# A two-layer hybrid transformer block: tail steps by banks, sums of squares on GpSimd, the inverse's matrices on VectorE, more turns for differential attention

## The chip, the cores and the metric

The kernel runs on one core of one Trainium2 chip. The metric is the device time of one execution in microseconds, as the median of several runs. A core has TensorE (PE in the profile, its weight loads PEld), VectorE (DVE), ScalarE (ACT), GpSimd (POOL) and SyncE (SP), which issues the DMAs. Each engine executes its own instructions in a fixed order and waits on semaphores for the others.

## The reference

x is 256 tokens by 1024. Each of two layers applies a feed-forward block, a mixer and a second feed-forward block, each with a norm before and a norm after it:

```python
for l in range(DEPTH):
    h = _rms_norm(x, ffn1_norm_pre[l])
    x = x + 0.5 * _rms_norm(_swiglu(h, ...), ffn1_norm_post[l])
    h = _rms_norm(x, mix_norm_pre[l])
    m = _mixer(h, w_in[l], ...)          # z = h @ w_in; three branches; gates; @ w_out
    x = x + _rms_norm(m, mix_norm_post[l])
    h = _rms_norm(x, ffn2_norm_pre[l])
    x = x + 0.5 * _rms_norm(_swiglu(h, ...), ffn2_norm_post[l])
```

`_swiglu` is `(silu(h @ w_gate) * (h @ w_up)) @ w_down` with an inner width of 2816. The mixer's branches are a sparse attention (top 64 keys by an index score), a linear recurrence (RWKV-7: a 64x64 state per head, updated by one rank-one correction per token), and differential attention: two softmaxes per head, p1 - lam * p2, times v, and a norm. All is float32.

## The kernel before, in words

**Tiling.** The 256 tokens are two halves t = 0 and 1 of 128. A matmul with weights of 512 or 1024 columns is cut into steps of 1024 weight values per partition. Each step's weights arrive by DMA in `raw`, and are split into a high part `wh` (a cast on ScalarE) and a rest `wl` (a subtraction on VectorE), both at line 224. A product is three matmuls, lines 233 to 235 (`mm3`): high by low, high by high, and `wl` by high. An output of 1024 columns fills two PSUM banks of 512.

**Order of steps.** `run_skew` (line 238) walks through a list of steps. The first `head` ones run for t = 0 and then for t = 1, the middle ones for both t in turn, and the last `tail` ones for t = 0 and then for t = 1. The last matmul of each stage (w_down, or w_out in a mixer) has a tail of EXTRA = 7 steps, whose weights are held for both t in extra buffers. A step of the tail does both banks before the next step. So t = 0 has its norm calculated while t = 1 is still multiplied. The transposes that the next stage needs (`rest`, line 356, PE line 362) are put into PE's order by `later`, ahead of the last step.

**Stage end.** `post_norm` (line 384) calls `rstd` (line 323): two squares with sums on ScalarE (line 330), their sum on VectorE (332), a power on GpSimd (333). Then for each half `y = ps * rstd * g` (391) and `x = y * factor + x` (392). `pre_norm` repeats `rstd` on the new x and makes `xn` (353), which PE transposes.

**The mixer's middle.** Three generators are advanced by `tick`, one turn after each step: sparse attention, differential attention (`diff`, line 740) and the recurrence. The recurrence inverts triangular matrices in `rwkv_solve` (line 996). After a small solve on VectorE and a passage through DRAM (`zs`, `xs`), four block-diagonal matrices `Z` are built on VectorE (line 1032), and two matrices `T` on GpSimd (1036) in the same turns as the first two Z. Then come three levels: `L` by Z on PE (line 193 through `mm`), masked to `W` on VectorE (1063), T by W on PE, and the addition to Z (1074). `diff` makes scores on PE, adds a mask (767), has a softmax over ScalarE and VectorE (653 to 656), combines both maps (773, 774) and, after LAG = 2 turns, transposes `lm` (line 196 through `tpose`) for the product with v. It does so for two head pairs of t = 0 and then of t = 1.

A scheduler puts instructions into each engine's order by priority: norms first (`pn`), weight loads and splits next (`p0`), then the generators' work (`p1`); `behind` keeps some of them after a given instruction.

Of the kernel before, what the change touches and what calls it, by code (L numbers as in the profile page):

```python
# [8 lines left out]
F32 = mybir.dt.float32  # L9
# [3 lines left out]
OP = mybir.AluOpType  # L13
# [6 lines left out]
EPS = 1e-6  # L20
# [3 lines left out]
LAG = 2  # L24
# [15 lines left out]
class Block:  # L40
# [197 lines left out]
    def run_skew(self, steps, head=0, tail=0):  # L238

        n = len(steps)  # L240
        order = [(t, i) for t in range(2) for i in range(head)]
        order += [(t, i) for i in range(head, n - tail) for t in range(2)]
        order += [(t, i) for t in range(2) for i in range(n - tail, n)]
        held = {}
        for j, (t, i) in enumerate(order):
            if self.later and (head and j == head - 1 or tail and j == len(order) - 1):
                self.later.pop(0)()
            if t == 0:
                wait = RING <= i < head or i >= n - tail
                held[i] = steps[i][0](self.extra if wait else self.ring)  # L250
            steps[i][1](t, held[i])
            self.tick()

    def steps_b(self, rows, n, ksteps, xk, psum, done=None):

        per = max(1, min(1024 // n, ksteps))
        steps, ps, raws = [], {}, {}
        nb = (n + 511) // 512

        def mk(k0):  # L260
            def ld(pool):
                if k0 % (2 * per) == 0:
                    kk = min(2 * per, ksteps - k0)
                    raws[0] = self.load(rows(k0, kk), kk, n)
                o = k0 % (2 * per)
                return self.split(raws[0][:, o:o + per, :], per, n, pool)

            def go(t, w):
                if k0 == 0:
                    ps[t] = [psum() for _ in range(nb)]  # L270
                for kk in range(per):
                    xh, xl = xk(k0 + kk, t)
                    for b in range(nb):
                        c0, c1 = b * 512, min(n, b * 512 + 512)
                        self.mm3(ps[t][b][:, :c1 - c0], xh, xl, w[0][:, kk, c0:c1], w[1][:, kk, c0:c1],
                                 k0 + kk == 0, k0 + kk == ksteps - 1, False)
                if k0 + per == ksteps and done is not None:
                    done(t, ps[t])
            return ld, go

        for k0 in range(0, ksteps, per):
            steps.append(mk(k0))
        return steps
# [39 lines left out]
    def rstd(self, parts, width):  # L323

        nc = self.nc
        ss = self.st.tile([128, 2], F32, name="ss")
        s = 1.0 / math.sqrt(width)
        for i, p in enumerate(parts):
            j = self.sq.tile([128, 512], mybir.dt.bfloat16, name="junk")
            nc.scalar.activation(j, p, AF.Square, scale=s, accum_out=ss[:, i:i + 1])  # L330
        r = self.st.tile([128, 1], F32, name="rstd")
        nc.vector.tensor_scalar(r, ss[:, 0:1], ss[:, 1:2], EPS, op0=OP.add, op1=OP.add)
        nc.gpsimd.tensor_tensor(r, r, self.mhalf[:, 0:1], op=OP.pow)
        return r

# [48 lines left out]
    def post_norm(self, t, ps, g, factor):  # L384
        nc = self.nc
        with self.pn():
            r = self.rstd(ps, D)
            for h in range(2):
                s = slice(h * 512, h * 512 + 512)
                y = self.junk.tile([128, 512], F32, name="xn")  # L390
                nc.vector.scalar_tensor_tensor(y, ps[h], r, g[:, s], op0=OP.mult, op1=OP.mult)
                nc.vector.scalar_tensor_tensor(self.x[t][:, s], y, factor, self.x[t][:, s], op0=OP.mult, op1=OP.add)
                if not self.phases:
                    nc.sync.dma_start(self.out[0, t * 128:t * 128 + 128, s], self.x[t][:, s])
        self.pre_norm(t)
# [344 lines left out]
    def diff(self, st, vd):  # L740
        nc = self.nc
        while "attended" not in st:
            yield
        q, k = st["dq"], st["dk"]
# [6 lines left out]
        for t in range(2):  # L751
# [5 lines left out]
            for h2 in range(2):  # L757
                lm = self.tp.tile([128, 1024], F32, name="lm", tag="lm", bufs=1)[:, :4 * S].rearrange(
                    "p (j s) -> p j s", s=S)
                yield  # L760
                pss = [self.bank(self.atp)[:, :2 * S].rearrange("p (j s) -> p j s", s=S) for _ in range(2)]
                for j in range(2):
                    for mp in range(2):
                        rw = slice(mp * 64, mp * 64 + 64)
                        self.mm(pss[mp][:, j, :], q[rw, 2 * h2 + j, ts], k[rw, 2 * h2 + j, :S], start=True, stop=True)
                for mp, ps in enumerate(pss):
                    nc.vector.scalar_tensor_tensor(lm[:, 2 * mp:2 * mp + 2, :], ps, 0.125,
                                                   self.cmS[:, None, o:].to_broadcast([128, 2, S]),
                                                   op0=OP.mult, op1=OP.add)
                rs = self.softmax(lm, 4, S, "d")  # L770
                for j in range(2):
                    p0, p1 = lm[:, j, :], lm[:, 2 + j, :]
                    nc.vector.tensor_scalar(p1, p1, rs[:, 2 + j:3 + j], lam, op0=OP.mult, op1=OP.mult)
                    nc.vector.scalar_tensor_tensor(p0, p0, rs[:, j:j + 1], p1, op0=OP.mult, op1=OP.subtract)
                for _ in range(LAG):
                    yield
                for s in range(t + 1):
                    yield
                    ps = self.bank(self.atp)[:, :256].rearrange("p (h c) -> p h c", c=128)
                    for j in range(2):  # L780
                        self.tpose(ps[:, j, :], lm[:, j, s * 128:s * 128 + 128], self.ident)
                    nc.scalar.copy((pt1 if s else pt0)[:, 2 * h2:2 * h2 + 2, :], ps)
# [7 lines left out]
            ss = self.st.tile([128, 4], F32, name="dss")  # L790
# [6 lines left out]
            for h in range(4):  # L797
                nc.vector.scalar_tensor_tensor(yt[:, h, :], ps[:, h, :], ss[:, h:h + 1], self.sub,
                                               op0=OP.mult, op1=OP.mult)
            yts.append(yt)  # L800
        for _ in range(2 * LAG):
            yield
        while self.gp is None:
# [192 lines left out]
    def rwkv_solve(self, Ls, strip):  # L996
# [32 lines left out]
        for q in range(4):  # L1029
            Zs.append(self.ep.tile([128, 4, 128], F32, name="Z", tag="s"))  # L1030
            with self.behind(self.attended):
                nc.vector.tensor_tensor(Zs[q].rearrange("p u (g x) -> p u g x", x=16),
                                        zs[:, 4 * q:4 * q + 4, None, :].to_broadcast([128, 4, 8, 16]), d16, op=OP.mult)
            if q < 2:
                Ts.append(self.ep.tile([128, 4, 128], F32, name="T", tag="s"))
                nc.gpsimd.tensor_tensor(Ts[q].rearrange("p v (g x) -> p v g x", x=16),
                                        xs[:, 4 * q:4 * q + 4, None, :].to_broadcast([128, 4, 8, 16]), even, op=OP.mult)
            yield


# [228 lines left out]
```

## Time and profile before

| what | value |
|---|---|
| median of 3 runs | 1435.26 us (1435.07, 1435.26, 1437.74) |
| the profiled execution's own time | 1437.46 us |
| its span in the profile | 1435.8 us |
| busy: PE, DVE, ACT, POOL | 1399.8, 1012.3, 713.2, 77.5 us |
| chain that ended last | PE 79%, DVE 9%, DMA 6%, ACT 3%, issue 2% |
| HBM traffic | 171 GB/s over the span |

Layer 0's mixer builds its Z at 362 us, layer 1's at 1072 us. Feed-forward and mixer stages end at about 197, 532, 718, 906, 1241 and 1430 us (the first five by the first transposes, line 362, of the next). The rows in the section below are single instructions or groups. In a timeline row a bracket gives the idle time of the engine before it and what ended it; in a table by stretches, "PEclk" is the granted TensorE clock as a share of full speed.

### The profile page before, as it was taken

To read this page: it belongs to the slowest core of one execution; us is meant where nothing else is said; L and a number is where in the kernel's file an instruction comes from. 1 tells how busy PE (TensorE), PEld (TensorE's weight loads), DVE (VectorE), ACT (ScalarE), POOL (GpSimd) and SP (SyncE) were. 2 spreads that over 40 slices of the span, in tenths; PEclk is the share of its full clock that TensorE was granted. 3 is DMA by queue.
4 is the path that set the end of the run, shared out by engine and by line. 5 is a ranking of instruction groups with operands and counts; after the bars stand their busy time and mean duration, and the time that the engine had idled before them with its cause. 6 is when DMAs were issued, how large, how long until landed. Compare 5 with 4: busy or idle time off the path is not lost.

```text
span 1435.8 us, 20311 instructions
## 1 busy us (share of the span) xinstructions
PE 1399.8 (97%) x8077; PEld 1203.1 (84%) x8077; DVE 1012.3 (71%) x1496; ACT 713.2 (50%) x1090; POOL 77.5 (5%) x92
## 2 busy tenths in 40 slices
PE   8999999999899999999999999999999999999997
PEld 5888879999688878888888888799887888788886
DVE  5777564988666877776567764659977668768753
ACT  5444454656463554444454444555545635544442
POOL 1000010121100000000000000100300000000000
PEclk9999999999999999999999999999999999999999
DMA  6665665455332564665646656554443326555653
GB/s 220 189 192 194 216 223 186 122 175 152 102 118 89 184 211 148 194 200 200 225 147 189 192 201 237 174 180 147 147 136 101 135 86 226 173 175 178 215 182 114
DMA packets 176407, 246.91 MB, mean 172 GB/s; under 512 B 17908, under 2 KB 128440, under 8 KB 176312
## 3 DMA queue, kind: packets, MB, share of 16 engines
q1 hardware_dynamic: 176312, 245.62, 52.6%
q8 instruction: 63, 1.03, 0.3%
q14 instruction: 32, 0.26, 0.1%
HBM read 241.80 MB, written 3.80 MB: 171 GB/s over the span
## 4 chain that ended last, share of the span: by engine, by line
PE 79%; DVE 9%; DMA 6%; ACT 3%; issue 2%; POOL 0%; SPq 0%; DVEq 0%; POOLq 0%; ACTq 0%
PE ps L310 28%; PE ps L233 11%; PE ps L235 11%; PE ps L234 11%; PE ps L193 7%; DVE wl L224 4%; PE ps L229 3%; PE ps L230 3%; PE ps L231 3%; ACT wh L224 2%; DMA raw<-in_w_in_dram 1%; DMA raw<-in_w_out_dram 1%; PE ps L196 1%; DMA zs<-d 1%; DMA raw<-in_ffn_w_gate_dram 1%
## 5 line engine op out<-in xcount | busy, mean ns | idle before, releaser
L224 DVE TENSOR_TENSOR wl<-raw,wh 128x1024 fp32r<-128x1024 f32 x438 | 531.8, 1222 | 240.4 <-ACT wh L224 239.2
L224 ACT CAST wh<-raw 128x1024 fp32r<-128x1024 f32 x438 | 452.9, 1045 | 453.3 <-PE ps L310 183.4
L310 PE MATMUL ps<-h,wh 128*128 128x512 f32 x1152 | 392.5, 393 | 0.0
L310 PE MATMUL ps<-h,wl 128*128 128x256 f32 x1152 | 300.2, 281 | 0.0
L310 PEld LDWEIGHTS ps<-h,wh 128*128 128x128 f32 x1152 | 206.1, 188 | 37.1
L310 PEld LDWEIGHTS ps<-h,wl 128*128 128x128 f32 x1152 | 216.9, 188 | 12.4
L233 PE MATMUL ps<-wh,h 128*128 128x512 f32 x384 | 160.0, 417 | 2.2 <-DVE h L224 1.9
L229 PE MATMUL ps<-h,wh 128*128 128x256 f32 (+1 forms) x560 | 158.6, 283 | 0.0
L230 PE MATMUL ps<-h,wh 128*128 128x256 f32 (+1 forms) x560 | 156.8, 280 | 0.0
L235 PE MATMUL ps<-wl,h 128*128 128x512 f32 x384 | 153.1, 399 | 2.8 <-DVE wl L224 2.8
L231 PE MATMUL ps<-h,wl 128*128 128x256 f32 (+1 forms) x560 | 155.7, 278 | 0.0
L234 PE MATMUL ps<-wh,h 128*128 128x512 f32 x384 | 152.2, 396 | 0.0
L233 PE MATMUL ps<-wh,gl 128*128 128x512 f32 x352 | 137.3, 390 | 0.0
L235 PE MATMUL ps<-wl,gh 128*128 128x512 f32 x352 | 137.0, 389 | 0.0
L234 PE MATMUL ps<-wh,gh 128*128 128x512 f32 x352 | 136.9, 389 | 0.0
L229 PEld LDWEIGHTS ps<-h,wh 128*128 128x128 f32 (+1 forms) x560 | 104.8, 187 | 2.0 <-issue 1.3
L230 PEld LDWEIGHTS ps<-h,wh 128*128 128x128 f32 (+1 forms) x560 | 104.9, 187 | 0.3
L231 PEld LDWEIGHTS ps<-h,wl 128*128 128x128 f32 (+1 forms) x560 | 104.7, 187 | 0.1
L235 PEld LDWEIGHTS ps<-wl,h 128*128 128x128 f32 x384 | 72.7, 189 | 22.6 <-DVE wl L224 5.6
L233 PEld LDWEIGHTS ps<-wh,h 128*128 128x128 f32 x384 | 72.5, 189 | 20.2 <-issue 3.3
L234 PEld LDWEIGHTS ps<-wh,h 128*128 128x128 f32 x384 | 72.8, 190 | 13.4
L235 PEld LDWEIGHTS ps<-wl,gh 128*128 128x128 f32 x352 | 66.1, 188 | 13.9
(272 smaller groups left out, 1715.0 us busy)
## 6 DMA issues: line engine op xcount, KB each, us to landing
raw<-in_w_in_dram SPq DMA_DIRECT2D x66, 1024.0 KB, 5.1
raw<-in_ffn_w_up_dram SPq DMA_DIRECT2D x44, 1024.0 KB, 5.4
raw<-in_ffn_w_down_dram SPq DMA_DIRECT2D x44, 1024.0 KB, 4.9
raw<-in_ffn_w_gate_dram SPq DMA_DIRECT2D x43, 1024.0 KB, 5.4
raw<-in_w_branch_dram SPq DMA_DIRECT2D x12, 1024.0 KB, 4.9
raw<-in_w_out_dram SPq DMA_DIRECT2D x8, 1024.0 KB, 5.6
gpre<-in_ffn_norm_pre_dram SPq DMA_DIRECT2D x4, 512.0 KB, 5.2
gpost<-in_ffn_norm_post_dram SPq DMA_DIRECT2D x4, 512.0 KB, 6.3
```

The costliest lines, as they stand in the source:

```text
L193: self.small = self.nc.tensor.matmul(*a, **k)
L196: self.small = self.nc.tensor.transpose(*a, **k)
L224: return self.nc.scalar.copy(hi, src), self.nc.vector.tensor_sub(lo, src, hi.bitcast(F32))
L229: mm(ps, wh, xl, start=first, stop=False)
L230: mm(ps, wh, xh, start=False, stop=False)
L231: self.last = mm(ps, wl, xh, start=False, stop=last)
L233: mm(ps, xl, wh, start=first, stop=False)
L234: mm(ps, xh, wh, start=False, stop=False)
L235: self.last = mm(ps, xh, wl, start=False, stop=last)
L310: self.last = mm(*a, start=k == i == 0, stop=k == 7 and i == 1)
```

## The change

(a) In the tail of `run_skew` each t does all steps of bank 0 and then all of bank 1; the matmul's `done` follows the last step of bank 1, and the transposes of `later` go in one place earlier in the new list. (b) In `rstd` the two partial sums are added on GpSimd, in front of the power. (c) `post_norm` first makes both `y = ps * factor * g`, and then `x = y * rstd + x`. (d) `diff` takes 2 * LAG turns in place of LAG between the softmax and the transposes, and one more turn after each yt. (e) `rwkv_solve` builds T on VectorE, in the turns of the third and fourth Z.

```diff
+        order += [(t, i, b) for t in range(2) for b in range(2) for i in range(n - tail, n)]
...
-            if self.later and (head and j == head - 1 or tail and j == len(order) - 1):
+            if self.later and (head and j == head - 1 or tail and j == len(order) - 2):
...
-            steps[i][1](t, held[i])
+            steps[i][1](t, held[i], b)
...
-                    for b in range(nb):
+                    for b in range(nb) if only is None else (only,):
...
-                if k0 + per == ksteps and done is not None:
+                if k0 + per == ksteps and done is not None and only in (None, nb - 1):
...
-        nc.vector.tensor_scalar(r, ss[:, 0:1], ss[:, 1:2], EPS, op0=OP.add, op1=OP.add)
+        nc.gpsimd.tensor_scalar(r, ss[:, 0:1], ss[:, 1:2], EPS, op0=OP.add, op1=OP.add)
...
+            ys = []
             for h in range(2):
+                y = self.junk.tile([128, 512], F32, name="xn")
+                nc.vector.scalar_tensor_tensor(y, ps[h], factor, g[:, h * 512:h * 512 + 512], op0=OP.mult, op1=OP.mult)
+                ys.append(y)
+            for h, y in enumerate(ys):
...
-                nc.vector.scalar_tensor_tensor(y, ps[h], r, g[:, s], op0=OP.mult, op1=OP.mult)
-                nc.vector.scalar_tensor_tensor(self.x[t][:, s], y, factor, self.x[t][:, s], op0=OP.mult, op1=OP.add)
+                nc.vector.scalar_tensor_tensor(self.x[t][:, s], y, r, self.x[t][:, s], op0=OP.mult, op1=OP.add)
...
-                for _ in range(LAG):
+                for _ in range(2 * LAG):
...
             yts.append(yt)
+            yield
...
-            if q < 2:
+            if q > 1:
                 Ts.append(self.ep.tile([128, 4, 128], F32, name="T", tag="s"))
-                nc.gpsimd.tensor_tensor(Ts[q].rearrange("p v (g x) -> p v g x", x=16),
-                                        xs[:, 4 * q:4 * q + 4, None, :].to_broadcast([128, 4, 8, 16]), even, op=OP.mult)
+                nc.vector.tensor_tensor(Ts[-1].rearrange("p v (g x) -> p v g x", x=16),
+                                        xs[:, 4 * q - 8:4 * q - 4, None, :].to_broadcast([128, 4, 8, 16]), even, op=OP.mult)
```

VectorE in layer 0's mixer, from the first Z to the combination of the first head pair's maps, before (`lm`, `nmd` and `smd` belong to the differential softmax):

```order
L1032 TENSOR_TENSOR Z<-zs,blk_1732 128x512 x3
L224 TENSOR_TENSOR wl<-raw,wh 128x1024
L1032 TENSOR_TENSOR Z<-zs,blk_1732 128x512
L767 SCALAR_TENSOR_TENSOR lm<-ps,cmS 128x256
L224 TENSOR_TENSOR wl<-raw,wh 128x1024
L767 SCALAR_TENSOR_TENSOR lm<-ps,cmS 128x256
L653 TENSOR_REDUCE nmd<-lm 128x4
L1063 TENSOR_TENSOR W<-ps,blk_1732 128x512 x2
L224 TENSOR_TENSOR wl<-raw,wh 128x1024
L656 RECIPROCAL smd<-smd 128x4
L773 TENSOR_SCALAR lm<-lm,smd,lam 128x128 x2
L774 SCALAR_TENSOR_TENSOR lm<-lm,smd 128x128 x2
```

The same place on VectorE after the change (line numbers are 4 or 5 higher there):

```order
L1037 TENSOR_TENSOR Z<-zs,blk_1732 128x512 x3
L224 TENSOR_TENSOR wl<-raw,wh 128x1024
L1041 TENSOR_TENSOR T<-xs,even 128x512
L1037 TENSOR_TENSOR Z<-zs,blk_1732 128x512
L224 TENSOR_TENSOR wl<-raw,wh 128x1024
L1041 TENSOR_TENSOR T<-xs,even 128x512
L771 SCALAR_TENSOR_TENSOR lm<-ps,cmS 128x256 x2
L1068 TENSOR_TENSOR W<-ps,blk_1732 128x512
L657 TENSOR_REDUCE nmd<-lm 128x4
L224 TENSOR_TENSOR wl<-raw,wh 128x1024
L1068 TENSOR_TENSOR W<-ps,blk_1732 128x512
L660 RECIPROCAL smd<-smd 128x4
```

Two T stand between the Z and the W, and the second W has come behind a weight split. On PE the transposes of lm, which stood some twenty rows behind the first Z products, stand some twenty rows later, behind the products of T and W.

VectorE from the last gated product to the transposed input of the next stage, at the end of layer 0's first feed-forward block, before:

```order
L224 TENSOR_TENSOR wl<-raw,wh 128x1024 x20
L332 TENSOR_SCALAR rstd<-ss 128x1
L391 SCALAR_TENSOR_TENSOR xn<-ps,rstd,gpost 128x512 x2
L392 SCALAR_TENSOR_TENSOR x_113<-xn,x_113 128x512 x2
L224 TENSOR_TENSOR wl<-raw,wh 128x1024
L332 TENSOR_SCALAR rstd<-ss 128x1
L224 TENSOR_TENSOR wl<-raw,wh 128x1024
L353 SCALAR_TENSOR_TENSOR xn<-x_113,rstd,gpre 128x512 x2
```

And after:

```order
L224 TENSOR_TENSOR wl<-raw,wh 128x1024 x18
L392 SCALAR_TENSOR_TENSOR xn<-ps,gpost 128x512
L224 TENSOR_TENSOR wl<-raw,wh 128x1024 x2
L392 SCALAR_TENSOR_TENSOR xn<-ps,gpost 128x512
L396 SCALAR_TENSOR_TENSOR x_113<-xn,rstd,x_113 128x512 x2
L224 TENSOR_TENSOR wl<-raw,wh 128x1024 x2
L354 SCALAR_TENSOR_TENSOR xn<-x_113,rstd,gpre 128x512 x2
```

The first y stands two splits earlier, both sums are gone from VectorE, and the splits stay around the chain.

PE in the first steps of that block's tail, before (`ps_1279` and `ps_1280` are the two banks of t = 0, the number behind `wh` and `wl` is the tile's):

```order
L235 MATMUL ps_1279<-wl_1534,gh7_181 128x512
L233 MATMUL ps_1280<-wh_1533,gl7_192 128x512
L234 MATMUL ps_1280<-wh_1533,gh7_181 128x512
L235 MATMUL ps_1280<-wl_1534,gh7_181 128x512
L233 MATMUL ps_1279<-wh_1545,gl8_193 128x512
L234 MATMUL ps_1279<-wh_1545,gh8_182 128x512
L235 MATMUL ps_1279<-wl_1546,gh8_182 128x512
```

After, where the pass over bank 0 (steps up to `wh_1581`) meets the pass over bank 1 (again from `wh_1533`):

```order
L233 MATMUL ps_1279<-wh_1574,gl10_195 128x512
L234 MATMUL ps_1279<-wh_1574,gh10_184 128x512
L233 MATMUL ps_1280<-wh_1533,gl7_192 128x512
L234 MATMUL ps_1280<-wh_1533,gh7_181 128x512
L235 MATMUL ps_1279<-wl_1575,gh10_184 128x512
L233 MATMUL ps_1279<-wh_1581,gl10_195 128x512
L234 MATMUL ps_1279<-wh_1581,gh10_184 128x512
L235 MATMUL ps_1280<-wl_1534,gh7_181 128x512
L233 MATMUL ps_1280<-wh_1542,gl8_193 128x512
L235 MATMUL ps_1279<-wl_1582,gh10_184 128x512
```

A few matmuls of bank 1 stand between the last ones of bank 0, ahead of those that need the newest `wl`.

## Rows read from the trace of the kernel before

**Rows 1.** PE's waits over the span: total us, times, longest.
```profile
PE ps L362 <- DVE xn L353: 5.6, 4, 2.0
PE ps L193 <- DVE Z L1032: 5.0, 5, 1.8
PE ps L196 <- DVE lm L774: 4.1, 2, 2.1
```

**Rows 2.** Two stretches of the mixers: length, each engine's busy us, PEclk, DMA share, GB/s.
```profile
362.00:380.00 18.00, 12.69 (x67) 9.94 (x66) 14.70 (x23) 5.05 (x15) 3.09 (x2) 0.91 0.37 117
1071.00:1089.00 18.00, 12.60 (x60) 10.13 (x60) 14.10 (x21) 4.63 (x14) 3.17 (x2) 0.81 0.36 117
```

**Rows 3.** PE's timeline there: start, us, engine, line, operation, [idle before <- releaser].
```profile
363.08 0.68 PE L193 MATMUL ps<-Z,up 128*128 128x128 f32 x4 [0.34 <-DVE Z L1032]
...
371.29 1.13 PE L193 MATMUL ps<-W,T 128*128 128x128 f32 x8 [1.04 <-DVE W L1063]
...
375.17 0.30 PE L196 MATMUL ps<-ident,lm 128*128 128x128 f32 x1 [2.05 <-DVE lm L774]
...
395.13 1.13 PE L193 MATMUL ps<-dk,dq 64*128 64x256 f32 x4 [0.66 <-DVE yt L798]
...
1073.02 0.68 PE L193 MATMUL ps<-Z,up 128*128 128x128 f32 x4 [1.76 <-DVE Z L1032]
```

**Rows 4.** VectorE's timeline in layer 0's mixer, and GpSimd's.
```profile
362.25 4.04 DVE L1032 TENSOR_TENSOR Z<-zs,blk 128x512 f32<-128x512 f32 x3 [4.67 <-DMA zs<-d]
...
367.35 0.68 DVE L1032 TENSOR_TENSOR Z<-zs,blk 128x512 f32<-128x512 f32 x1
...
370.46 1.28 DVE L1063 TENSOR_TENSOR W<-ps,blk 128x512 f32<-128x512 f32 x2
372.81 1.22 DVE L224 TENSOR_TENSOR wl<-raw,wh 128x1024 fp32r<-128x1024 f32 x1 [1.07 <-ACT wh L224]
...
362.65 3.09 POOL L1036 TENSOR_TENSOR T<-xs,even 128x512 f32<-128x512 f32 x2 [31.59 <-DMA xs<-d]
```

**Rows 5.** Timeline at the end of layer 0's mixer, all engines.
```profile
524.69 0.59 ACT L330 ACTIVATE junk<-ps 128x512 bf16<-128x512 f32 x1
...
525.96 0.21 DVE L332 TENSOR_SCALAR rstd<-ss 128x1 f32<-128x1 f32 x1
...
526.25 0.56 POOL L333 TENSOR_TENSOR rstd<-rstd,mhalf 128x1 f32<-128x1 f32 x1 [57.35 <-DVE rstd L332]
...
526.84 1.41 DVE L391 SCALAR_TENSOR_TENSOR xn<-ps,rstd,gpost 128x512 f32<-128x512 f32 x2 [0.67 <-POOL rstd L333]
...
532.23 0.63 PE L362 MATMUL ps<-ident,xn 128*128 128x128 f32 x4 [1.84 <-DVE xn L353]
```

**Rows 6.** Timeline at the end of layer 1's first feed-forward block.
```profile
903.78 1.22 DVE L224 TENSOR_TENSOR wl<-raw,wh 128x1024 fp32r<-128x1024 f32 x1
...
904.01 1.39 POOL L333 TENSOR_TENSOR rstd<-rstd,mhalf 128x1 f32<-128x1 f32 x1 [5.16 <-DVE rstd L332]
...
906.24 0.99 PE L362 MATMUL ps<-ident,xn 128*128 128x128 f32 x5 [1.96 <-DVE xn L353]
```

**Rows 7.** PE at the end of layer 1's mixer, and VectorE at the end of the kernel.
```profile
1240.99 0.63 PE L362 MATMUL ps<-ident,xn 128*128 128x128 f32 x4 [1.36 <-DVE xn L353]
...
1430.21 1.41 DVE L391 SCALAR_TENSOR_TENSOR xn<-ps,rstd,gpost 128x512 f32<-128x512 f32 x2 [0.73 <-POOL rstd L333]
```

**Rows 8.** Timeline in the tail of layer 1's first feed-forward block: weights and their use.
```profile
890.15 2.36 DVE L224 TENSOR_TENSOR wl<-raw,wh 128x1024 fp32r<-128x1024 f32 x2 [3.92 <-ACT wh L224]
...
893.70 0.39 PE L235 MATMUL ps<-wl,gh 128*128 128x512 f32 x1
...
895.06 0.39 PE L235 MATMUL ps<-wl,gh 128*128 128x512 f32 x1
```

**Rows 9.** VectorE's timeline in layer 0: softmax of the first head pair of t = 1.
```profile
395.59 1.40 DVE L767 SCALAR_TENSOR_TENSOR lm<-ps,cmS 128x512 f32<-128x512 f32 x2
397.02 1.22 DVE L653 TENSOR_REDUCE nmd<-lm 128x4 f32<-128x1024 f32 x1
```

More of the change, by code (lines that the diff above doesn't have):

```diff
@@ L240, in run_skew @@
         n = len(steps)
-        order = [(t, i) for t in range(2) for i in range(head)]
-        order += [(t, i) for i in range(head, n - tail) for t in range(2)]
-        order += [(t, i) for t in range(2) for i in range(n - tail, n)]
+        order = [(t, i, None) for t in range(2) for i in range(head)]
+        order += [(t, i, None) for i in range(head, n - tail) for t in range(2)]
+        order += [(t, i, b) for t in range(2) for b in range(2) for i in range(n - tail, n)]
         held = {}
-        for j, (t, i) in enumerate(order):
-            if self.later and (head and j == head - 1 or tail and j == len(order) - 1):
+        for j, (t, i, b) in enumerate(order):
+            if self.later and (head and j == head - 1 or tail and j == len(order) - 2):
                 self.later.pop(0)()
-            if t == 0:
+            if i not in held:
                 wait = RING <= i < head or i >= n - tail
                 held[i] = steps[i][0](self.extra if wait else self.ring)
-            steps[i][1](t, held[i])
+            steps[i][1](t, held[i], b)
             self.tick()
@@ L266, in ld, with go @@
                 return self.split(raws[0][:, o:o + per, :], per, n, pool)
-            def go(t, w):
+            def go(t, w, only):
                 if k0 == 0:
@@ L387, in post_norm @@
             r = self.rstd(ps, D)
+            ys = []
             for h in range(2):
+                y = self.junk.tile([128, 512], F32, name="xn")
+                nc.vector.scalar_tensor_tensor(y, ps[h], factor, g[:, h * 512:h * 512 + 512], op0=OP.mult, op1=OP.mult)
+                ys.append(y)
+            for h, y in enumerate(ys):
                 s = slice(h * 512, h * 512 + 512)
-                y = self.junk.tile([128, 512], F32, name="xn")
-                nc.vector.scalar_tensor_tensor(y, ps[h], r, g[:, s], op0=OP.mult, op1=OP.mult)
-                nc.vector.scalar_tensor_tensor(self.x[t][:, s], y, factor, self.x[t][:, s], op0=OP.mult, op1=OP.add)
+                nc.vector.scalar_tensor_tensor(self.x[t][:, s], y, r, self.x[t][:, s], op0=OP.mult, op1=OP.add)
                 if not self.phases:
```

## The prediction

> **What bounds the kernel now.** The table of the profile, read first, has PE busy for 1399.8 of 1435.8 us: PE's program sets the time, and a change that leaves PE's instructions as they are can gain only where PE waits or has its clock halved. So I read the list of PE's waits next [rows 1]: the reader is to see that the three largest, 5.6, 5.0 and 4.1 us, are for xn at stage ends, for Z, and for lm, and that this change touches the path to each. Then a table by stretches of the two mixer middles, where Z and lm lie [rows 2]: of 18.00 us PE is busy for 12.69 (layer 0) and 12.60 (layer 1), so idle for 5.31 and 5.40. The granted clock is 0.91 and 0.81 of full there; the lost share is 18 x 0.09 = 1.62 us and 18 x 0.19 = 3.42 us. Third, the timelines of PE and VectorE in these places [rows 3 to 7], to find which producer ends each wait last.
>
> **T on VectorE (e) and lm later (d): the mixer's middle.** Before, three Z take 4.04 us, 1.3 each, while GpSimd builds two T in 3.09 us at the same time; the fourth Z, alone, takes 0.68 [rows 4]. Two W of the same 128x512, with one operand in PSUM, take 1.28, or 0.6 each in succession [rows 4]. So I read the first Z as slowed by the T beside it, not by their own work. With T on VectorE after them, three Z are 3 x 0.6 = 1.9 us and two T cost 2 x 0.6 = 1.2 us: VectorE's row to the last T becomes 2.2 - 1.2 = 1.0 us shorter, and, what matters more, PE's second product has its Z1 at 363.5 instead of 364.7.
>
> The second piece is the largest single gap, 2.05 us in each layer: PE stood at the transpose of lm [rows 3], which VectorE completed after a split that itself had waited 1.07 us for ScalarE [rows 4]. With 2 * LAG turns the transposes come some twenty PE rows later, behind the T-by-W products, and PE does not meet lm unfinished. What is late next is W: I laid the new VectorE row out by hand with the durations above and 1.14 us for each split (Z0 to Z2 at 362.25 to 364.1, split, T0 to 365.8, Z3 to 366.5, split, T1 to 368.2, two masks of 0.34, W0 to 369.5). PE then waits 0.34 for Z0, 0.13 for Z1, 0.7 for Z3, 1.1 for W0, nothing for lm, and 0.15 in place of 0.66 for yt [rows 3], since the extra turn parts both. That is 2.4 us in layer 0; in layer 1, where Z0 comes 1.76 us late by its DMA [rows 3], 3.8 us.
>
> No half clock is left in this estimate: in both layers it was granted just after the lm gap, and in layer 1 also after the Z gaps of 1.76 and 0.98, and the remaining gaps are shorter and apart. Gains: layer 0, 5.31 + 1.62 + 0.66 - 2.4 = 5.2; layer 1, 5.40 + 3.42 + 0.66 - 3.8 = 5.7. In the second half of the solve differential attention's work comes later and denser; I allow 0.4 us a layer for new waits there. **Sum of the middles: 10.1 us**; bounds: 6.5 (one half clock of 1.7 left in each layer) to 11.5.
>
> **Stage ends (a, b, c).** At the end of layer 0's mixer the last square is at 524.69, the sum 0.21 us, the power 0.56, two y 1.41, and then both x [rows 5]; PE waits 1.84 us at the transposes. Both y leave the path, since they no longer need rstd: two successive y are 1.41, of which 1.33 stands between the power and x. Squares of bank 0 come seven steps earlier, so ScalarE has one operation fewer in front of the last square: 0 to 0.5 us gained, 0.1 taken. Against it the sum on GpSimd: no row has this operation there. Nearest above is the power with two operands of the same 128x1, 0.56; from below, VectorE's 0.21 [rows 5]. I take 0.45, nearer to the power as the same engine's, so 0.25 more than before. Net 1.33 + 0.1 - 0.25 = 1.2 us, and a little from the sum of pre_norm that no longer queues behind a split: 1.3 of the 1.84. At the end of layer 1's mixer PE waits 1.36 us [rows 7], and I take 1.3. At the end of layer 1's first feed-forward block the wait is 1.96 [rows 6], but there x is late by weight splits too, and the power takes 1.39 beside a split; I take half of 1.3, 0.64. At the kernel's end [rows 7] nothing hides the chain; ScalarE already overlaps the first square with the last matmuls there: 1.33 - 0.25 = 1.08. The other stage ends have no wait of this kind. **Sum of the stage ends: 4.3 us**, bounds 1.5 to 5.5.
>
> **What the tail by banks costs.** A step now stays 0.68 us on PE in the first pass instead of 1.36 (two successive uses of wl, 893.70 and 895.06 [rows 8]), so step j of the tail is wanted 0.68 x j earlier, 3.4 and 4.1 us for the last two weights that arrive. In the tightest tail, layer 1's first block, their splits end at about 891.4 and at 890.15 + 2.36 = 892.5, so 2.3 and 2.55 us before that use [rows 8]: short by 1.1 and 1.5. PE's order has matmuls of bank 1 as fillers there, two and four of them at 0.23 us, which give 0.45 and 0.9 back; 0.63 us is left, and the xn wait of 1.96 behind it absorbs that. In the other three feed-forward tails the splits lie 0.4 to 0.8 us earlier before their use, which by the same reckoning leaves 0.26, 0.07 and nothing. 0.33 us in all, or 4.4 without the fillers. The mixers' tails read shorter matrices and have over 5 us of slack. Start-up, which also has new sums on GpSimd, but waits for x by DMA: 0 +- 0.25. **Cost 0.35 us.**
>
> **The sum** against the profiled execution's own 1437.46: 1437.46 - 10.1 - 4.3 + 0.35 = **1423.4 us**. The median of the runs shown, 1435.26, is 2.2 us lower. If those 2.2 are part of what goes (layer 1's later Z and its second half clock are 1.4 and 1.7 dearer than in layer 0 [rows 2, 3]), the median run also ends at 1423.4; if not, at 1421.2. I take 1422.
>
> **A rule to weigh.** The timeline shows a power of 0.56 us in one place [rows 5] and of 1.39 in another, where a split runs on VectorE: it ends 0.4 us after the split's end [rows 6]. The Trainium skill, page "SBUF — State Buffer", section "SBUF: two separate sides", says that VectorE and GpSimd share one pair of ports as an exclusive lock, which a VectorE operation with two SBUF inputs holds for all its length. The slowed Z and the slowed power agree with that; by that rule part (b) is a risk, because now two GpSimd operations in a row can be caught by a split, and the time would be rival 1's, 1424.5, in place of 1422.
>
> **The rivals.**
> 1. *GpSimd's sum is caught.* The splits stay around the chain at stage ends. One more catch costs 1.39 - 0.56 = 0.83 us; with three chains on the path, 2.5 us: 1422 + 2.5 = 1424.5. For it: rows 6. Against: at the kernel's end and after the first x no split runs. Chance 0.11.
> 2. *The middle keeps a clock drop* or an unforeseen wait of about 1.7 us in each layer: 1422 + 1.7 to 3.4, about 1425 to 1426. For it: 1.1 + 0.7 us of waits remain in my layout, next to each other. Chance 0.17.
> 3. *Z is slow of itself* (two SBUF inputs with repeated operands), and T on VectorE costs 1.2 to 1.7 each. Then each layer loses 2 x 1.2 + 1 = 3.4 us against the forecast: about 1429. Against: the fourth Z, alone, 0.68. Chance 0.07.
> 4. *Given back*: the diff's products end later than the phase behind them allows, or the weights of the tails stall as without fillers (4.4) and the middles keep half: within 3 us of before, 1434. Chance 0.06.
> 5. *Slower*: differential attention's softmax for t = 1 sits on VectorE ahead of the recurrence's state updates. Of one head pair it is 1.40 + 1.22 [rows 9] + 0.18 + 0.73 + 0.88 = 4.4 us, and with the wait for ScalarE's exponentials in it 7.3. If the delayed turns put both pairs into the serial chain of the recurrence, where before they ran beside it, each layer gives back more than 7 us; from there on the gain of 14 is gone, and with a clock drop of 1.7 in each layer it is 1422 + 14.6 + 3.4 = 1440. For it: they are four turns later for each of four pairs. Against: PE still has projections to do in every turn there. Chance 0.06.
>
> **How the numbers follow.** The forecast, both gains with a plain cover, has 0.53, with its own range 1418 to 1425. The range that should hold 8 in 10 goes up to rival 3, 1430, and down to the better ends of both sums (10.1 to 11.5, 4.3 to 5.5, lower by 2.6 together, and the clock of the median run), 1417; outside lie rivals 4 and 5 and a few of the rest. A measurement of this kernel can tell about 0.2%, 2.9 us, from no change: faster has 0.53 + 0.11 + 0.17 + 0.07 = 0.88 less 0.01 of rival 3's upper end, 0.87; the same 0.07; slower 0.06.
>
> **What would show it.** Right: three Z in about 2 us and T of 0.6 to 0.7 on VectorE; no PE wait on lm; waits for Z and W of under 1.2 us each; a clock of 0.97 or more in both stretches; x starting right after the power at the stage ends, and about 6.2 us from the last square to the first transpose at the end of layer 0's mixer, where it was 532.23 - 524.69 = 7.5. Wrong: T of over 1 us; a GpSimd sum of over 0.8; waits on wl in the tails of over 1 us; new waits over 1 us in the recurrence behind 380 us in layer 0, above all on VectorE's state updates, with a lm operation in front of them.

## The result, and the profile after

The changed kernel takes **1422.01 us** (median of 4 runs, 1420.35 to 1425.62) beside 1436.5 for the kernel before (4 runs, 1435.07 to 1440.2): a ratio of 0.9904, 95% interval 0.9876 to 0.9931. Two later jobs gave 1420.47 (0.9900, interval 0.9876 to 0.9923) and 1419.42 (0.9908, interval 0.9886 to 0.9929). The profiled execution took 1422.70, with a span of 1421.0. The forecast was 1422. That the first median agrees to 0.01 us is chance, as the medians of the three jobs lie 2.6 us apart; the gain that was added up, 14.1 of 1437.46, is a ratio of 0.9902, and the three measured ratios are 0.9900 to 0.9908.

PE's waits in the changed kernel, as in [rows 1] (line numbers are 1 to 5 higher):

```profile
PE ps L235 <- DVE wl L224: 2.7, 3, 1.7
PE ps L363 <- DVE xn L354: 2.0, 3, 1.3
PE ps L193 <- DVE Z L1037: 2.0, 3, 1.1
PE ps L233 <- DVE h L224: 1.9, 2, 1.0
PE ps L193 <- DVE W L1068: 1.7, 2, 0.8
...
PE ps L193 <- DVE yc L1184: 1.6, 2, 0.8
...
PE ps L193 <- DVE lk L1126: 1.1, 2, 0.5
```

The three waits of [rows 1] summed to 14.7 us. The one for lm is gone, those for xn and Z are 2.0 each, and two new ones have come, for yc and lk, 2.7 together (yc and lk are intermediate results of the recurrence). Of the 2.0 us for xn, 1.25 are at the start of the kernel, where it was 0.48; at the stage ends 5.16 us have become 0.74.

The stretches of [rows 2], moved to where the same work now lies (363.60 to 381.60 has PE busy for the same 16.63 us), and a third one around 302 us:

```profile
361.00:379.00 18.00, 16.63 (x98) 13.31 (x98) 14.00 (x25) 7.83 (x20) 0.00 (x0) 1.00 0.51 136
1064.00:1082.00 18.00, 15.64 (x100) 12.89 (x99) 15.32 (x27) 8.56 (x20) 0.00 (x0) 1.00 0.37 117
299.00:307.00 8.00, 6.98 (x47) 6.78 (x46) 4.94 (x8) 5.46 (x11) 3.36 (x3) 0.79 0.64 214
```

PE is idle for 1.37 and 2.36 us of 18, where it was 5.31 and 5.40, and has its full clock in both. In this execution it was granted half its clock in another place, behind a wait of 1.02 us for sq (squares for the recurrence, made on ScalarE) at 300 us: 8 x 0.21 = 1.7 us.

VectorE at the place of [rows 4], and PE at that of [rows 3]:

```profile
363.88 1.90 DVE L1037 TENSOR_TENSOR Z<-zs,blk 128x512 f32<-128x512 f32 x3 [4.66 <-DMA zs<-d]
365.69 1.22 DVE L224 TENSOR_TENSOR wl<-raw,wh 128x1024 fp32r<-128x1024 f32 x1
366.83 0.69 DVE L1041 TENSOR_TENSOR T<-xs,even 128x512 f32<-128x512 f32 x1
...
368.26 0.68 PE L193 MATMUL ps<-Z,up 128*128 128x128 f32 x4 [0.42 <-DVE Z L1037]
...
371.17 1.16 PE L193 MATMUL ps<-W,T 128*128 128x128 f32 x8 [0.82 <-DVE W L1068]
...
436.00 1.10 PE L193 MATMUL ps<-ar,bk 64*128 64x256 f32 x4 [0.78 <-DVE yc L1184]
...
441.88 1.13 PE L193 MATMUL ps<-ar,bk 64*128 64x256 f32 x4 [0.54 <-DVE lk L1126]
```

Three Z take 1.90 us where they took 4.04, and T costs 0.69 at most. The waits of 0.78 and 0.54 lie in the recurrence, 65 us later.

The end of layer 0's mixer, as in [rows 5]: ScalarE, GpSimd, VectorE, PE.

```profile
517.86 2.00 ACT L224 CAST wh<-raw 128x1024 fp32r<-128x1024 f32 x2 [0.64 <-DMA raw<-in_ffn_w_gate_dram]
519.76 0.58 ACT L331 ACTIVATE junk<-ps 128x512 bf16<-128x512 f32 x1
...
520.54 0.93 POOL L333 TENSOR_SCALAR rstd<-ss 128x1 f32<-128x1 f32 x1 [55.37 <-ACT junk L331]
521.55 0.57 POOL L334 TENSOR_TENSOR rstd<-rstd,mhalf 128x1 f32<-128x1 f32 x1
...
522.15 1.42 DVE L396 SCALAR_TENSOR_TENSOR xr<-xn,rstd,xr 128x512 f32<-128x512 f32 x2 [0.25 <-POOL rstd L334]
...
526.45 0.63 PE L363 MATMUL ps<-ident,xn 128*128 128x128 f32 x4 [0.17 <-DVE xn L354]
```

x follows the power directly, and from the last square to the first transpose it is 526.45 - 519.76 = 6.7 us, where it was 7.5 and the prediction named 6.2. The wait is 0.17 us. The first row is one that the prediction didn't stop at: the square stands behind casts that wait for the next stage's weights.

GpSimd and VectorE at the end of the kernel, as in [rows 7]:

```profile
1416.05 0.56 POOL L334 TENSOR_TENSOR rstd<-rstd,mhalf 128x1 f32<-128x1 f32 x1
1416.65 1.41 DVE L396 SCALAR_TENSOR_TENSOR xr<-xn,rstd,xr 128x512 f32<-128x512 f32 x2 [0.35 <-POOL rstd L334]
```

Here, too, x follows the power, and the time behind the last matmul is 6.21 us, where it was 7.35.

The first transposes of each stage, and those of t = 1, can be used as landmarks. By them, the 14.76 us between the two profiled executions divide as follows. Layer 0's mixer with its end: 532.23 - 209.43 before, 526.45 - 209.48 after, 5.83 less. Layer 1's: 1240.99 - 918.41 and 1227.23 - 911.61, 6.96 less. Layer 1's first block with its second norm: 918.41 - 730.48 and 911.61 - 724.82, 1.14 less. Behind 1240.99 and 1227.23: 1.00 less, of which the time behind the last matmul has 1.14. The rest: 0.17 more.

### The profile page after: what moved, and what is told of

It is laid out like the page before. It is cut to its first block, busy times and chain, and to the rows that moved or that the text cites. A ratio compares the mean times of both kernels' runs of the same rounds, so it can differ in the third digit from the quotient of the medians.

```text
span 1421.0 us, 20363 instructions
## 1 busy us (share of the span) xinstructions
PE 1396.2 (98%) x8077; PEld 1200.1 (84%) x8077; DVE 1006.2 (71%) x1476; ACT 713.6 (50%) x1090; POOL 84.4 (6%) x112
## 3 DMA queue, kind: packets, MB, share of 16 engines
q8 instruction: 63, 1.03, 0.3%
```

## The experiments

The changed kernel is the base of all of them but the sixth, which is told apart. Each result is told by places in its profile too, since the runs of one kernel scatter by 2 to 6 us.

**T back on GpSimd.**

```diff
-            if q > 1:
+            if q < 2:
-                nc.vector.tensor_tensor(Ts[-1]...xs[:, 4 * q - 8:4 * q - 4...
+                nc.gpsimd.tensor_tensor(Ts[-1]...xs[:, 4 * q:4 * q + 4...
```

> Only part (e) is undone: T is built on GpSimd in the turns of the first two Z again. Theory (Z is slowed by the T beside it): three Z take about 4.0 us in place of 1.9, GpSimd's T 1.5 each; PE waits for Z about 0.3 + 1.0 + 0.9 us in layer 0 in place of 0.42, and some 1.4 us more in layer 1; no wait for lm; 1.5 to 2.5 us a layer longer, a span of 1424 to 1426 us against 1421.0. Rival (Z is slow of itself when it starts behind its DMA, and it was the later turns that made the first three fast): Z x3 stays near 1.9 and the span within 1 us of 1421.

Median 1426.0 us (7 runs), ratio 0.9944, interval 0.9927 to 0.996. The profiled execution, 1433.96, had other waits on top (2.5 us for sq, 1.8 for ml), so its span says nothing; the six others were 1425.6 to 1427.1, with spans of 1423.9 to 1425.4, about as the theory had it. VectorE, GpSimd and PE in its first mixer:

```profile
366.79 4.04 DVE L1037 TENSOR_TENSOR Z<-zs,blk 128x512 f32<-128x512 f32 x3 [4.62 <-DMA zs<-d]
...
367.17 3.12 POOL L1041 TENSOR_TENSOR T<-xs,even 128x512 f32<-128x512 f32 x2 [31.66 <-DMA xs<-d]
...
369.30 0.68 PE L193 MATMUL ps<-Z,up 128*128 128x128 f32 x4 [0.99 <-DVE Z L1037]
372.72 0.68 PE L193 MATMUL ps<-Z,up 128*128 128x128 f32 x4 [0.90 <-DVE Z L1037]
```

The same three Z take 4.04 again, while all the rest of the change stands. So Z was slowed by T beside it, and that rival falls. There is no wait for lm, so part (e) is not what removed that one.

**The turns of differential attention back.**

```diff
-                for _ in range(2 * LAG):
+                for _ in range(LAG):
...
             yts.append(yt)
-            yield
```

> Only part (d) is undone: LAG turns ahead of the transposes of lm, and no extra turn after yt. Theory (PE met lm before VectorE had it, and the turns removed that): PE waits for lm again, 1 to 2.5 us in each layer, since T now also stands on VectorE ahead of it, with a half clock behind it; the waits for yc and lk behind 430 us go; 2 to 4 us a layer longer, a span of 1425 to 1429. Rival (part (e) alone freed VectorE early enough, and the turns only bring the new waits of 1.3 us a layer): the wait for lm stays under 0.5 us and the span is 1418 to 1421.

Median 1425.75 us (4 runs), ratio 0.9933, interval 0.9914 to 0.9952. PE in layers 0 and 1:

```profile
373.17 0.30 PE L196 MATMUL ps<-ident,lm 128*128 128x128 f32 x1 [1.62 <-DVE lm L778]
...
1076.22 0.30 PE L196 MATMUL ps<-ident,lm 128*128 128x128 f32 x1 [1.64 <-DVE lm L778]
```

The wait for lm is back in both layers, without a half clock behind it; those for yc and lk are gone. So the turns remove 1.6 and the 0.66 for yt, and bring 1.3. In the profile the two mixers are only 1.1 and 1.0 us longer than in the changed kernel's. The first figure needs two corrections: the changed kernel had lost 1.7 us there to the half clock at 302 us, and this one waits 1.27 us for ml (the low parts of w_out's input), which the kernel with tails by steps, below, has with the turns in place (1.2); that leaves about 1.5. Both are under the 2 to 4 expected. The medians are 3.7 us apart, but this kernel's runs alone span 4.0.

**Tails by steps again.** (The order of `run_skew` and the place of `later` as in the kernel before.)

```diff
-        order += [(t, i, b) for t in range(2) for b in range(2) for i in range(n - tail, n)]
+        order += [(t, i, None) for t in range(2) for i in range(n - tail, n)]
```

> Only part (a) is undone: the tails go by steps, both banks in each. Theory (the early square of bank 0 is worth a little at each stage end, and the price is stalls in the feed-forward tails): the wait of 0.67 us for wh in the tail of layer 1's first block goes; at the stage ends the last square comes up to 0.5 us later and the first one of t = 0 5 us later; PE's waits for xn grow by 0.3 to 1 us at the ends of the two mixers and at 900 us; span 1421.0 + 0.3 to 2. Rival (the tail order is what the stage ends gained from): the xn waits come back to over 1.2 us each, and the span is 1424 to 1426.

1424.31 us in one run, a span of 1422.6. The waits for xn at the mixers' ends are 0.49 and 0.76 in place of 0.17 and 0.57; at 900 us there is none, and the wait for wh in that tail is gone too. But from the first transposes of t = 0 to those of t = 1 it takes 0.4 to 0.65 us longer at each of the five inner ends, with waits for wl of 0.17 to 0.37 us that the changed kernel does not have. Of the 1.6 us more, 1.2 is a wait for ml at 513 us, which the kernel with the turns put back, whose tails go by banks, has too (1.3). So beside the other parts, part (a) is worth 0.2 to 0.3 us in the wait at each mixer's end and about half a microsecond behind each inner end. The rival falls. What part (a) costs does not follow from the wait for wh: all three profiles of the changed kernel have it (0.67, 0.77 and 1.88 us), but none of the seven other kernels here whose tails go by banks does.

**The sums on VectorE.**

```diff
-        nc.gpsimd.tensor_scalar(r, ss[:, 0:1], ss[:, 1:2], EPS, op0=OP.add, op1=OP.add)
+        nc.vector.tensor_scalar(r, ss[:, 0:1], ss[:, 1:2], EPS, op0=OP.add, op1=OP.add)
```

> Only part (b) is undone: VectorE adds the two square sums again. Theory (a sum on GpSimd is caught by a weight split just as the power was before, so that the move is worth nothing at most ends): the powers are 0.56 in one place and 1.39 beside a split, as in the kernel before, and PE's waits for xn change by less than 0.5 us each, in either direction; span 1420.5 to 1422. Rival (the sum on VectorE stands behind a split and is late by up to 1.2 us): waits for xn of over 1 us at 900 us and at the mixers' ends, span 1422.5 to 1425.

1423.65 us in one run, a span of 1421.9. The time behind the last matmul falls from 6.21 to 6.09. Of the 24 powers five take over 1 us. At layer 1's mixer end PE waits 2.30 us for xn, with a half clock behind it; that is 1.7 more than in the changed kernel, so the theory's 0.5 did not hold there, and it looks like the rival. ScalarE, VectorE and GpSimd there, and then ScalarE and GpSimd of the changed kernel:

```profile
1218.08 2.00 ACT L224 CAST wh<-raw 128x1024 fp32r<-128x1024 f32 x2 [2.02 <-DMA raw<-in_ffn_w_gate_dram]
1219.99 0.58 ACT L331 ACTIVATE junk<-ps 128x512 bf16<-128x512 f32 x1
...
1221.44 0.21 DVE L333 TENSOR_SCALAR rstd<-ss 128x1 f32<-128x1 f32 x1
...
1221.73 0.56 POOL L334 TENSOR_TENSOR rstd<-rstd,mhalf 128x1 f32<-128x1 f32 x1 [58.35 <-DVE rstd L333]
```

```profile
1218.36 2.00 ACT L224 CAST wh<-raw 128x1024 fp32r<-128x1024 f32 x2 [0.68 <-DMA raw<-in_ffn_w_gate_dram]
1220.26 0.59 ACT L331 ACTIVATE junk<-ps 128x512 bf16<-128x512 f32 x1
...
1222.05 0.57 POOL L334 TENSOR_TENSOR rstd<-rstd,mhalf 128x1 f32<-128x1 f32 x1
```

From the square's start to the power it is 1.74 us; in the changed kernel it is 1.79. The sum is no later on either engine. What made the wait is the first row: PE had come 2.5 us earlier to this place than in the changed kernel's profile (1224.15 against 1226.65). The load that the casts waited for was issued 2.3 us earlier, too (1210.31 against 1212.62), but its cast began only 0.3 us earlier, and the square stands behind it.

**y behind rstd again.**

```diff
-                nc.vector.scalar_tensor_tensor(y, ps[h], factor, g[:, h * 512:h * 512 + 512], ...)
...
-                nc.vector.scalar_tensor_tensor(self.x[t][:, s], y, r, self.x[t][:, s], ...)
+                nc.vector.scalar_tensor_tensor(y, ps[h], r, g[:, s], ...)
+                nc.vector.scalar_tensor_tensor(self.x[t][:, s], y, factor, self.x[t][:, s], ...)
```

> Only part (c) is undone: post_norm multiplies ps by rstd again, so both y stand between the power and x. Theory (two y leave the path, 1.3 us at each stage end on the path): the time behind the last matmul of the kernel goes from 6.2 to 7.3-7.5 us; PE's waits for xn grow from 0.2 and 0.6 to 1.5 and 1.9 us at the two mixers' ends, and a wait of about 1 us comes at 900 us; span 1424 to 1425.5. Rival (at the ends inside the kernel it is ScalarE's squares, held up behind weight casts that wait for their DMA, that decide, and they shift the time more than the y): only the 1.1 us at the kernel's end are sure, and the waits inside differ from the changed kernel's by less than 0.7 us each; span 1422 to 1423.

1432.93 us in one run: more than either theory said. The time behind the last matmul is 7.42, as forecast. The waits for xn are 1.26 and 0.51 at the mixers' ends, between the two, and 0.24 at 902 us, where the theory had about 1. But PE also waits 1.5 us for a wl in the first steps behind both first feed-forward blocks, which neither theory had. VectorE and PE in layer 0:

```profile
207.94 1.41 DVE L354 SCALAR_TENSOR_TENSOR xn<-x,rstd,gpre 128x512 f32<-128x512 f32 x2 [0.85 <-POOL rstd L334]
209.28 1.22 DVE L224 TENSOR_TENSOR wl<-raw,wh 128x1024 fp32r<-128x1024 f32 x1
...
210.55 0.50 PE L235 MATMUL ps<-wl,h 128*128 128x512 f32 x1 [1.48 <-DVE wl L224]
```

VectorE at the same place of the changed kernel:

```profile
203.22 3.49 DVE L224 TENSOR_TENSOR wl<-raw,wh 128x1024 fp32r<-128x1024 f32 x3
207.46 1.41 DVE L354 SCALAR_TENSOR_TENSOR xn<-x,rstd,gpre 128x512 f32<-128x512 f32 x2 [0.76 <-POOL rstd L334]
```

One split is queued on VectorE behind xn, which waits for a longer chain; with part (c) the order has all three splits ahead of xn there. That is 2.0 us at each of the two. Waits of 0.7 and 1.9 us for ml, the second with a half clock behind it, came on top; they are not explained by this part.

**Parts (d) and (e) alone** (the three parts undone above, together).

> Parts (d) and (e) alone; tails, sums and post_norm are those of the kernel before. Theory (the middles are worth 10 us and the stage ends 4, and they add up): median 1425 to 1427.5, waits for xn of 1.3 to 2.5 us at the two mixers' ends and at 905 us as in the kernel before, 7.35 us behind the last matmul. Rival (what the middles gain is lost again at the mixers' ends without the shorter chain, because the weights of the next stage arrive by DMA at their own time): waits for xn of over 3 us at the mixers' ends, median 1428 to 1431.

Median 1427.14 us (5 runs, 1422.56 to 1428.42), ratio 0.993, interval 0.9905 to 0.9956; the changed kernel in the same job 1420.47. The theory's number came: a ratio of 0.993 is 10 us for the middles. The waits did not come as it had them, 1.3 to 2.5 at three places: at the mixers' ends they are 2.98 and 0.94, and at 900 us there is none. PE's timeline at the two mixers' ends, and two stretches there with its clock as the third number from the end:

```profile
527.04 1.08 PE L363 MATMUL ps<-ident,xn 128*128 128x128 f32 x4 [2.98 <-DVE xn L354]
...
1215.71 0.53 PE L233 MATMUL ps<-wh,ml 128*128 128x512 f32 x1 [1.87 <-DVE ml L224]
```

```profile
526.00:530.00 4.00, 2.96 (x11) 2.67 (x12) 2.10 (x3) 1.15 (x2) 0.10 (x1) 0.57 0.00 0
1216.00:1220.00 4.00, 4.00 (x12) 3.11 (x12) 2.61 (x3) 1.65 (x2) 0.00 (x0) 0.57 0.83 262
```

The wait for xn is 2.98 where it was 1.84 [rows 5]: over 1 us of what the middle gains is lost at its own mixer's end, and a half clock with it. That is the rival's mechanism, in layer 0 alone.

The end of layer 1's first block says something about the parts that are undone here. ScalarE before, and ScalarE and PE here:

```profile
894.59 2.00 ACT L224 CAST wh<-raw 128x1024 fp32r<-128x1024 f32 x2 [3.52 <-DMA raw<-in_w_in_dram]
896.49 0.59 ACT L330 ACTIVATE junk<-ps 128x512 bf16<-128x512 f32 x1
```

```profile
889.20 2.00 ACT L224 CAST wh<-raw 128x1024 fp32r<-128x1024 f32 x2 [1.91 <-DMA raw<-in_w_in_dram]
891.67 0.60 ACT L331 ACTIVATE junk<-ps 128x512 bf16<-128x512 f32 x1 [0.47 <-PE ps L235]
...
900.33 1.32 PE L363 MATMUL ps<-ident,xn 128*128 128x128 f32 x8
```

Before, the square stood behind casts that had waited 3.52 us for weights; here the weights come earlier and the square waits for PE. The wait of 1.96 us for xn [rows 6] is gone without parts (a) to (c), though the power there takes 1.40 us beside a split as before. From t = 1's transposes of one stage to those of the next the block takes 187.93 us before, 185.81 here and 186.79 in the changed kernel. Why the weights come earlier is open, and with one profile of the kernel before it isn't known whether they are late there each time.

**Twice the turns for t = 0 alone.**

```diff
-                for _ in range(2 * LAG):
+                for _ in range(LAG if t else 2 * LAG):
```

> The changed kernel with 2 * LAG turns only for the head pairs of t = 0, whose transposes PE had waited for, and LAG for those of t = 1. Theory (the new waits for yc and lk, 1.3 us in each layer, come from t = 1 being four turns later): both waits go or fall under 0.3 us, a median of 1419 to 1420.5. Rival (the waits are the recurrence's own and only became visible, or t = 1 needs the turns as t = 0 does): they stay, or a wait for lm at the transposes of t = 1 takes their place; median 1421 to 1424.

Median 1423.57 us (4 runs), ratio 0.9915, interval 0.9892 to 0.9938. In layer 0 the wait for yc is gone, and those for lk are 0.77 and 0.19 in place of 0.54, so 0.4 us of 1.3 is saved. At its end PE waits 2.11 us for xn, with a half clock behind it: the load that the square stands behind was issued at 510.18, 2.3 us earlier than in the changed kernel's profile (512.45), and its cast began at 517.64, 0.2 us earlier (517.86). The rival's median came, 3.1 us above the changed kernel's of the same job, and the waits for lk stay, as it had it; that for yc goes when t = 1's turns are put back.

**The changed kernel again.**

> The changed kernel again, beside the others of this job. Median 1420.5 to 1424 as first measured. The half clock at 302 us, behind a wait of 1.0 us for sq, is expected again if a wait of that length brings it each time, and not again if it depends on where the wait falls.

Median 1420.47 us (4 runs). The wait for sq at 300 us was 0.83 us and no half clock followed it, where 1.02 had brought one. Over all profiles a wait of 1.02, 1.16 and 1.19 us there was followed by one, and a wait of 1.03, 1.19 and, in the kernel before, 1.62 was not. One of 2.52 us, in the kernel with T back on GpSimd, was followed by one of twice the length. So the length alone doesn't tell.

**Squares first.** `split` of the next stage is put behind the last square of t = 0 in the mixers' `post_norm`.

```diff
-        with self.p0(), self.behind(*(self.first if self.last is None else ())):
+        with self.p0(), self.behind(self.hold, *(self.first if self.last is None else ())):
...
             r = self.rstd(ps, D)
+            if t == 0 and factor == 1.0:
+                self.hold = self.sqr
```

> The changed kernel, with the next stage's first weight splits put behind the squares of t = 0 at the two mixers' ends. Theory (there ScalarE's squares stand behind casts that wait for the next weights' DMA, so the DMA's landing decides when xn is there): the second square ends within 1 us of the last matmul of t = 0, some 2 to 3 us earlier than in the changed kernel, PE's waits for xn at the mixers' ends go to zero in every execution, the median falls by 0.5 to 2 us against the changed kernel in this job and its highest run by more. Rival (the chain is bound by PE's matmuls and the norm's own length): no difference over 0.5 us, or a loss from weights that come later in the next stage.

**And mh first.** w_out's splits from its fifth step on are put behind mh and ml, too. (`late` does this for a step's load; its definition is left out here.)

```diff
+        steps[8:] = [(late(ld), go) for ld, go in steps[8:]]
```

> The same, and w_out's third and fourth loads are split behind the casts of the last merged halves (mh, ml). Theory (PE's occasional wait of 0.5 to 1.9 us for ml at the start of w_out comes from a split that waits for its DMA ahead of ml): no wait for ml over 0.3 us; a further 0 to 1 us in the median, more in the highest run. Rival (the weights themselves are as late): a wait for wh or wl takes the place of that for ml.

> The changed kernel beside these two, for comparison. Median 1420 to 1422.5 us, with waits for xn of 0.2 to 0.6 us at the mixers' ends unless a DMA lands late.

Medians of 6 runs each in one job: 1420.62 (1419.33 to 1422.92), 1419.25 (1418.48 to 1420.57), and the changed kernel 1419.42 (1417.67 to 1422.79); ratios 0.9916, 0.9904 and 0.9908 to the kernel before, with intervals of +-0.002. The changed kernel's median is under the 1420 to 1422.5 expected, and in its profile PE waits for xn at layer 1's end alone (0.28). So no gain that can be told, though the mechanism shows; both expected the median to fall. ScalarE, GpSimd and VectorE at layer 0's end with squares and mh first:

```profile
515.58 0.60 ACT L331 ACTIVATE junk<-ps 128x512 bf16<-128x512 f32 x1 [2.32 <-PE ps L235]
...
520.57 1.69 POOL L333 TENSOR_SCALAR rstd<-ss 128x1 f32<-128x1 f32 x1 [3.25 <-ACT junk L331]
...
518.68 3.49 DVE L224 TENSOR_TENSOR wl<-raw,wh 128x1024 fp32r<-128x1024 f32 x3
522.95 1.42 DVE L354 SCALAR_TENSOR_TENSOR xn<-xr,rstd,gpre 128x512 f32<-128x512 f32 x2 [0.77 <-POOL rstd L334]
```

The square now waits for PE, not for a cast, and x stands at 517.35, 3 us earlier than in the changed kernel's repeat (520.42). But the splits that were put back have come into the next norm: its sum on GpSimd takes 1.69 us beside them, and xn is only 0.9 us earlier than there (523.82). In the changed kernel's profile of the same job x stands at 519.77 and xn at 523.18, 2.4 and 0.2 us later. The first of the two versions still waits 0.88 us for xn at both ends, so its expectation of none failed; the second waits 0.20 us there. It has no wait for ml, but neither have the first version and the two repeats of the changed kernel, so that shows nothing. Its runs have the narrowest spread of the three. The changed kernel's profile in this job shows how large the wait for wh in layer 1's first block can be; PE there, and a stretch behind it:

```profile
883.48 0.50 PE L233 MATMUL ps<-wh,gl 128*128 128x512 f32 x1 [1.88 <-ACT wh L224]
```

```profile
885.00:888.00 3.00, 3.00 (x8) 2.33 (x8) 0.81 (x1) 0.42 (x1) 0.00 (x0) 0.50 0.37 82
```

That is 1.88 us and a half clock in this execution, 0.67 and 0.77 without one in the two others of this kernel.

## Why the prediction was right

| step | forecast | two profiled executions |
|---|---|---|
| middles, layers 0 and 1, after the allowance | 4.8 and 5.3 | 5.83 - 1.67 = 4.2 and 6.96 - 0.79 = 6.2 |
| mixers' ends, waits for xn | 1.3 and 1.3 | 1.84 - 0.17 = 1.67 and 1.36 - 0.57 = 0.79 |
| layer 1's first block | 0.64 | 1.14 |
| behind the last matmul | 1.08 | 1.14 |
| elsewhere | -0.35 | -0.3 |
| sum | 14.1 | 14.76 |

The middles came as they were added up. By the stretches, with yt before and yc and lk after, layer 0's gained 5.31 + 1.62 + 0.66 - 1.37 - 1.32 = 4.9 us and layer 1's 5.40 + 3.42 + 0.66 - 2.36 - 1.32 = 5.8, where 4.8 and 5.3 were forecast. The 4.2 in the table is lower by the half clock at 302 us, 1.7, less shorter waits for sq (1.62 to 1.02) and ml (0.49 to none). The row of layer 1's first block has its gain for another reason than the prediction gave, as the sixth experiment shows: the wait of 1.96 us goes with parts (a) to (c) undone, and the block is then 1 us shorter still than with them.

**T on VectorE**: right. Z of 0.6 beside nothing, T of 0.68 to 0.69, and with T back on GpSimd three Z take 4.04 us again. **lm later**: right in kind; undone alone, 1.6 us a layer of wait return.

**Waits left in the middle**: mis-sized, and better than forecast. I laid out 2.4 and 3.8 us; it is 1.37 and 2.36 in the stretches. In layer 0 Z0 and Z1 came without a wait (0.34 and 0.13 forecast), Z3 cost 0.42 in place of 0.7, and W0 0.82 in place of 1.1. That Z0 cost nothing there is luck, as PE came later by the half clock; in the second profile of this kernel it costs 0.54. **New waits in the second half**: mis-sized, and worse: 0.4 a layer forecast, 0.78 + 0.54 = 1.32 measured, where the row of VectorE has differential attention's work for t = 1 between the recurrence's mean and the first yc. That is the slower rival's mechanism at a fifth of the 7 us that it needs. Putting those turns back for t = 1 alone won 0.4 of them, and the median did not show it.

**No half clock is left**: right for the counted places, in all three profiles of the change. It did not hold for the kernel as a whole: one profile has one at 302 us, one has two others (in the start, and behind the wait for wh), one has none. The forecast had no term for these.

**The sum on GpSimd**: 0.45 forecast, 0.30 measured where nothing runs beside it, 0.70 to 1.76 beside a split, 0.78 in the mean of 24. Over 0.8 was one of the prediction's own signs of being wrong. The power behind it is now 0.56 or 0.57 each time (mean 842 ns before, 563 after): the sum takes the block that the power took. It also takes blocks that the power did not have: 11 of 24 sums are over 0.6 us, where 8 of 24 powers were before and 5 of 24 with the sums on VectorE. At the mixers' ends the sum was caught (0.93) and the power before had not been (0.56), so rival 1's catch came there, though its price was 0.93 - 0.30 = 0.63 and not 0.83. From the last square to the end of the power it is 2.36 us in layer 0, where it was 2.12; the 0.24 more is the 0.25 that the sum had. At the kernel's end part (b) costs 0.1 us by the fourth experiment; elsewhere that one run shows neither a gain nor a loss of it. The block agrees with the Trainium skill, page "SBUF — State Buffer", section "SBUF: two separate sides", that the two engines hold their shared ports by an exclusive lock. A second catch in the same chain, of the power, did not come in any of the 24: at layer 0's mixer end the split is over at 521.30, before the power starts at 521.55.

**y first**: 1.33 forecast; 7.42 - 6.21 = 1.2 at the kernel's end. At the mixers' ends 1.67 and 0.79 were measured for 1.3 each, and that the two agree in sum is luck, since what the square waits for there is the landing of the next stage's weights, ahead of it in ScalarE's order, which the prediction's sum does not have. With the square freed of it, x came 2.4 to 3 us earlier. Part (c) also has an effect that I did not see: without it the new tail has a split waiting behind xn, 2.0 us behind each of two blocks.

**Tail by banks**: 0.63 us of stall in the tightest tail forecast, to be absorbed by the wait for xn behind it; 0.67, 0.77 and 1.88 in the three profiles of the changed kernel. It is paid, not absorbed, since that wait is gone without part (a) as well: with tails by steps there is neither, and the block gains 1.85 us where the changed kernel gains 1.14. But the stall does not follow from the order alone. It is missing in the seven other kernels with tails by banks, whose blocks are 1.7 to 2.3 us shorter than before, but for the one with y behind rstd again; what brings it is open.

## What to carry to other kernels

When PE waits for an operand that VectorE builds, look at what GpSimd does in the same microseconds: here the same multiplication cost 1.3 us beside its twin on GpSimd and 0.6 alone, and moving the twin behind it on the busier engine was the better order. At a stage's end, look at what stands ahead of the norm in its engine's order: here a square stood behind casts that waited for the next stage's weights, so that coming 2.3 us earlier brought a wait of 2 us and almost no gain. A wait that is gone after a change need not be gone by it; the kernel with the other parts alone showed that for one of them. And where runs scatter by 2 to 6 us, read a part's gain from stretches between fixed landmarks.

## What the runs showed of the hardware

Whether a half clock follows a wait of PE could not be told from the wait's length: it followed some of 1.02 to 1.19 us and not others, it followed one of 1.88, and it did not follow 1.62 and 1.64 in the second experiment. At the start of the kernel it followed a wait of 2.07 us in one execution of the changed kernel and not one of 2.08 in another. Those ahead of the last matmul lasted 3.41 us, at a cost of 1.7, but for the one behind 2.52 us, which lasted 6.83.

The second load of 1 MB for the next gate took from 5.2 us (the changed kernel's first repeat) to 7.8 us (sums on VectorE) from its issue to the start of the cast that waited for it. That spread is as large as the waits at the mixers' ends.
